# A two-layer decoder trunk on one Trainium2 core: a place of its own for one half's residual, and later transposes, sums and gates in the convolution layer

## The chip, the cores and the metric

The kernel runs on one core of a Trainium2 chip. The metric is the device time of one execution in microseconds (us). A core has five engines that each work through their own list of instructions in order: TensorE (PE; its weight loads are shown as PEld), VectorE (DVE), ScalarE (ACT), GpSimd (POOL) and SyncE (SP), which here issues the DMAs. They meet through semaphores. A measurement of this kernel tells a difference of about 0.2% from none.

## What is computed

The input is 1024 tokens of 1024 channels in float32. Two layers follow each other; each has a token mixer and a feed-forward part with squared ReLU, and each of these four is followed by a residual and a layer norm. The first layer's mixer is a gated recurrence (HGRN2). The change lies in the second layer, whose mixer is a causal convolution module:

```python
u = h @ w_pw1 + b_pw1
a, gate = jnp.split(u, 2, axis=-1)
u = a * jax.nn.sigmoid(gate)
u = lax.conv_general_dilated(u, w_dw[:, None, :], ..., feature_group_count=D_MODEL) + b_dw   # 31 taps per channel
u = jax.nn.silu(layer_norm(u, ln_g, ln_b))
mix = u @ w_pw2 + b_pw2
x = layer_norm(DEEPNORM_ALPHA * x + mix, ln_mix_g[i], ln_mix_b[i])
ff = jnp.square(jax.nn.relu(x @ ffn_w1[i])) @ ffn_w2[i]
x = layer_norm(DEEPNORM_ALPHA * x + ff, ln_ffn_g[i], ln_ffn_b[i])
```

## The kernel before

Float32 products are made of three matmuls: every operand is split into a high part and a remainder (`split`: a cast on ACT, a subtraction on VectorE). A call of `product` (L327) issues one group of them into a PSUM bank, 24 matmuls of 128 x 512 for eight channel blocks or 12 for four. The two feed-forward parts use Strassen-like forms: sums and differences of weight blocks, some of which are formed on POOL by `pool_sums` (L443). That routine loads four weight blocks into four buffers, adds them in four steps and stores each result to DRAM.

The tokens are worked on in two halves of 512. `SEQ` (L38) is an order written by hand in which the stages of the second layer follow each other; a letter names the stage and the digit the half, the channel block or the chunk:

- `P0`, `P1` (`pointwise`, L1140): the gated first product of a channel block of the first and second half. It starts a convolution job: 19 taps on VectorE (`convolve`, L1188) and 12 whose products are scaled on ACT and added on POOL (`convolve_pool`, L1167); the two sums are added at L1204.
- First half: each convolved block is transposed back on TensorE and copied (`back`, L1219), so that tokens stand in the partitions, into the tile `ct[0]`. `N0` (`normalise`, L1236) applies the mean and deviation. `F0` (`finish`, L1301) transposes block by block again, applies gain, bias and silu and splits the result into `sT[0]` (`one(j)` for the eight blocks j). After the last block the residual `kept[0]`, stored in DRAM earlier, is loaded by four DMAs into `ct[0]` (L1318), one for each block of 128 tokens. `S0` (`second`, L1322) scales it and adds the bias (L1327), multiplies `sT[0]` by `w_pw2`, adds the products (L1349), normalises (`norm`, L721) and transposes the outcome into `x3T[0]` (`back` at L1333).
- Second half: the sums stay with the channels in the partitions, in `ct[1]` (`by_channel`, L1185). For their statistics TensorE transposes pairs of blocks into PSUM, where VectorE reads them (`measured`, L1207). `F1` (`second_half`, L1264) queues `stats` (the averages of L1255, with a power on POOL at L1260), `spread` (two groups of matmuls that spread the mean and the scale over the partitions, then eight multiplications on VectorE and eight additions on POOL, L1284, and at the end one `pool_sums` for a chunk of `w2`, L1286) and the silu of block pairs. `S1` is the second product of that half; it reads its residual from `ct[1]` again (L1296).
- `UA` and `UB`: up-projection of the second feed-forward part for the two halves, `V`, `W`, `X`, `Z` parts of its last two chunks in Strassen form. Before `UB0` the sums of `w1b` for these chunks are formed with `pool_sums` (L1524), whose copies read a column of `x3T[1]`.

`ct[0]` lies at 32 KB and `ct[1]` at 48 KB of each partition (L1136). The working order between engines is set by three things. A planner in the kernel (`Background`, L204) keeps estimated clocks of TensorE, VectorE and POOL. After each `product` it runs one entry of a list of chores (`bg.chore`), then steps of the convolution jobs as far as the clocks allow (`bg.pump`). A list `late` holds transposes to be issued inside a later convolution job, at its 6th (first half) or 10th tap (second half). Beyond that, the framework places every instruction in its engine's fixed list by its own schedule, where a later instruction that is expected to be ready may pass an earlier one. To hold a DMA back, the kernel writes one column of its target by a small POOL copy that reads the thing to wait for; `pool_sums` does so with its argument `after` (L449).

Of the kernel before, what the change touches and what calls it, by code (L numbers as in the profile page):

```python
# [8 lines left out]
F32 = mybir.dt.float32  # L9
# [6 lines left out]
P = 128  # L16
D = 1024
S = 1024
KB = D // P
H = 8  # L20
HT = 512
NTB = HT // P
# [238 lines left out]
def body(ctx, tc, d, out):  # L261
    nc = tc.nc
# [29 lines left out]
    def raws(kbs, name="raw"):  # L292
        return ring(kbs, (1024,), name)
# [21 lines left out]
    bg = Background()  # L315
    vector = Clocked(nc.vector, bg.dve, vector_cost)
    tensor = Clocked(nc.tensor, bg.pe, tensor_cost)
# [46 lines left out]
    ident = cst.tile([P, P], F32, name="ident")  # L364
# [325 lines left out]
    def half_stats(bs, yt, j):  # L690
        vector.bn_stats(bs[:, j], yt[:, j * HT : (j + 1) * HT])
# [79 lines left out]
    for half in range(2):  # L771
        for t in range(NTB):
            gates(1, half, t, ws)
        for h in range(H):
            pt = aux()
# [357 lines left out]
    big = Room(((144, 176), (216, 220)), {"u": ((PAD + HT,), 6), "r": (wide_t, 2), "cb": (wide_t, 4), "prod": (wide_t, 3), "z": (wide_t, 2), "halo": ((KB, PAD), 1)})  # L1133
    cvs = bank((3, 7))
    halo = big("halo")
    ct = [view(32 + 16 * h, (NTB, D), F32, "y") for h in range(2)]  # L1136
    cs, conv, pooled, late = [None, None], [], [], []
    taken, turned, gate, normed = [0], [0], [None, []], [0]

# [43 lines left out]
                yield  # L1183

    def by_channel(j):  # L1185
        return ct[1][:, j // 2, j % 2 * HT : (j % 2 + 1) * HT]

    def convolve(half, j, u, sums, other):  # L1188

        while half > normed[0]:  # L1190
            yield WAIT
        ca = cvs()
        if gate[1]:
            nc.vector.tensor_copy(out=ca[:, :1], in_=gate[1].pop())
        nc.scalar.activation(ca, u[:, :HT], AF.Identity, bias=par[:, BDW + j : BDW + j + 1], scale=tap(j, 0))  # L1195
        for i in range(1, TAPS - NPOOL):
            if i == (10 if half else 6):
                while late:
                    late.pop(0)()
            vector.scalar_tensor_tensor(out=ca, in0=u[:, i : i + HT], scalar=tap(j, i), in1=ca, op0=ALU.mult, op1=ALU.add)  # L1200
            yield
        bg.flush(other)
        cb = sums["cb"]
        vector.tensor_tensor(out=by_channel(j) if half else cb, in0=ca, in1=cb, op=ALU.add)  # L1204
        yield

        def measured():  # L1207

            if j == 1:
                cs[1] = stat.tile([P, NTB, 4, 6], F32, tag="cs", name="cs", bufs=1)  # L1210
            for t in range(0, NTB, 2):
                pt = rings["aux"]().rearrange("p (a b) -> p a b", a=2)
                for a in range(2):
                    for b in range(2):
                        tensor.transpose(pt[:, a, b * P : (b + 1) * P], by_channel(j - 1 + b)[:, (t + a) * P : (t + a + 1) * P], ident)
                for a in range(2):
                    vector.bn_stats(cs[1][:, t + a, j // 2], pt[:, a])

        def back():  # L1219
            pt = aux()  # L1220
            for t in range(NTB):
                tensor.transpose(pt[:, t, :], cb[:, t * P : (t + 1) * P], ident)
            nc.scalar.copy(out=ct[half][:, :, j * P : (j + 1) * P], in_=pt)
            turned[0] += 1
            if j % 4 == 3:
                if j == 3:
                    cs[half] = stat.tile([P, NTB, 4, 6], F32, tag="cs", name="cs", bufs=1)[:, :, :2]
                for t in range(NTB):
                    half_stats(cs[half][:, t], ct[half][:, t, :], j // 4)

        if half:
            turned[0] += 1
        if half == 0 or j % 2:
            late.append(measured if half else back)

    def normalise(half):  # L1236

        for job in conv[KB * half : KB * half + KB]:
            bg.flush(job)
        if half == 1:  # L1240
            return
        while late:
            late.pop(0)()
        mv = averages(half)
        normed[0] = 1
        gate[1] = [mv[:, 0, 4:5]] * 2
        for n in range(2):
            for t in range(NTB):
                cv = ct[half][:, t, n * HT : (n + 1) * HT]
                if n == 0 and t % 2:  # L1250
                    vector.tensor_scalar(out=cv, in0=cv, scalar1=mv[:, t, 3:4], scalar2=mv[:, t, 4:5], op0=ALU.mult, op1=ALU.add)
                else:
                    nc.scalar.activation(cv, cv, AF.Identity, bias=mv[:, t, 4:5], scale=mv[:, t, 3:4])
# [10 lines left out]
    def second_half():  # L1264

        at = {}

        def stats():
            while late:
                late.pop(0)()  # L1270
            at["mv"] = averages(1)

        def spread():

            for i, name in ((3, "scale"), (4, "mean")):
                at[name] = pt = banks[:, (3, 7)[i - 3]]
                for t in range(NTB):
                    tensor.matmul(pt[:, t * P : (t + 1) * P], at["mv"][:, t, i : i + 1].to_broadcast([P, P]), ident, start=True, stop=True)
            m = big("z")
            nc.scalar.copy(out=m, in_=at["mean"])  # L1280
            for j in range(KB):
                c = by_channel(j)
                vector.tensor_tensor(out=c, in0=c, in1=at["scale"], op=ALU.mult)
                nc.gpsimd.tensor_tensor(out=c, in0=c, in1=m, op=ALU.add)  # L1284

            pool_sums(*to_sum.pop(0), raws((144, 148, 152, 161), "four"))  # L1286

        def one(j):
            c, sg = by_channel(j), big("r")
            gj, bj = par[:, CLG + j : CLG + j + 1], par[:, CLB + j : CLB + j + 1]  # L1290
            nc.scalar.activation(sg, c, AF.Sigmoid, bias=bj, scale=gj)
            nc.scalar.activation(c, c, AF.Identity, bias=bj, scale=gj)
            vector.tensor_tensor(out=c, in0=c, in1=sg, op=ALU.mult)
            split(sT[1][:, 0, j, :], sT[1][:, 1, j, :], c)
            if j % 2:
                nc.sync.dma_start(out=ct[1][:, j // 2, :], in_=kept[1][j // 2])  # L1296

        nothing = lambda: None
        bg.chores += [stats, spread, nothing, *(lambda j=j: (one(j), one(j + 1)) for j in range(0, KB, 2))]

    def finish(half):  # L1301

        st = sT[half]

        def one(j):
            pt = rings["aux"]()
            for t in range(NTB):
                tensor.transpose(pt[:, t * P : (t + 1) * P], ct[half][:, t, j * P : (j + 1) * P], ident)
            z = big("z")
            sg = big("r")  # L1310
            gj, bj = par[:, CLG + j : CLG + j + 1], par[:, CLB + j : CLB + j + 1]
            nc.scalar.activation(sg, pt, AF.Sigmoid, bias=bj, scale=gj)
            nc.scalar.activation(z, pt, AF.Identity, bias=bj, scale=gj)
            vector.tensor_tensor(out=z, in0=z, in1=sg, op=ALU.mult)
            split(st[:, 0, j, :], st[:, 1, j, :], z)
            if j == KB - 1:
                for t in range(NTB):
                    nc.sync.dma_start(out=ct[half][:, t, :], in_=kept[half][t])  # L1318

        bg.chores += [lambda j=j: (one(j), one(j + 1)) for j in range(0, KB, 2)]  # L1320

# [168 lines left out]
    for op, i in steps:  # L1490
# [9 lines left out]
        if op in ("P0", "P1"):  # L1500
            pointwise(int(op[1]), i)
        elif op == "N":
            normalise(i)
        elif op == "F":
            if i == 1:

                rings["aux"] = bank((0, 4, 3, 7))
            second_half() if i else finish(i)
        elif op == "S":
            second(i)  # L1510
        elif op == "UA":
            up_half(1, i, 0, wa, stA, x3T[0])
        elif op in AHEAD:
            late_ahead(i, AHEAD[op])
        elif op == "Z":
            late_rest()
        else:
            if i == 0:
                wa.raws = raws((184, 188))
                drop(wa_last[1])  # L1520

                four = raws((132, 136, 140, 216), "four")
                for c in range(LATE):
                    pool_sums("w1b", 0, c, four, x3T[1][:, 1, KB - 1, 3 * P - 1 : 3 * P].bitcast(F32))  # L1524
                wa.plan([form("w1b", 0, c, j) for j in LATE_ORDER for c in range(LATE)])
                stB = {"hr": ring(run(0, 2, 16), (8, 2, 256), "hb"), "r": ring(run(128, 2, 2), wide_t, "r"), "t": ring(run(112, 4, 4), (2, 2, 256), "ht")}
            if i == 2:
                x4 += ring((132, 136, 140, 216), (2, HT), "x4", F32R).views
                tmp = ring(run(176, 4, 2), wide_t, "xt")
                for k in range(4):  # L1530
                    bg.chores += x3_differences(k, tmp)
            up_half(1, i, 1, wa, stB, x3T[1])


    y = ct
# [95 lines left out]
```

## Time and profile before

| | us |
|---|---|
| three runs, median | 2132.28 |
| lowest and highest of them | 2131.18, 2132.79 |
| the profiled execution | 2131.32 |
| its span, first to last instruction | 2129.5 |
| TensorE busy in it | 2108.3 |
| VectorE, ACT, POOL busy | 1534.3, 971.4, 451.5 |

A line of the timeline gives the start in us from the beginning of the span, the time until the last of its instructions has ended, the engine, the line of the kernel (L196 and L77 are helpers through which many operations go), the operation, what it writes and reads by tile names, their shapes, and how many instructions were merged (x). Brackets at the end hold the idle time of the engine just before and what ended it. Tiles have names of their own in it: `xa` and `xb` are the split inputs (`x2T`, `sT`) of the two halves, `xc` is `x3T[1]`, `y` stands for `ct`, `four` for the buffers of `pool_sums`, `cb` for POOL's convolution sum. SPq and POOLq rows are DMA issues.

### The profile page before, as it was taken

Reading aid. Unit: us, or ns where it says so; the run is one execution under the profiler, and the core shown is the slowest. Engines: PE = TensorE matmul, PEld = TensorE weight load, DVE = VectorE, ACT = ScalarE, POOL = GpSimd, SP = SyncE. Lnnn points to the kernel's source line nnn. Section 1 sums busy time; section 2 is a strip of 40 time slices with the busy share of each in tenths; the row PEclk is TensorE's granted clock in tenths of the full one; section 3 lists DMA queues with packets and bytes.
Section 4 is the critical chain, followed back from the end, with each engine's and each line's share of the span. In section 5 each row is a group of like instructions: output and inputs, shape, how many; then the busy total and the mean of one; then the engine's idle time right before and its main releaser. Section 6 shows DMA issues by size and latency. Waiting matters only on the chain. (4 is left out here: it accounts for less than half of the span.)

```text
span 2129.5 us, 27331 instructions
## 1 busy us (share of the span) xinstructions
PE 2108.3 (99%) x10136; PEld 1753.2 (82%) x10136; DVE 1534.3 (72%) x2208; ACT 971.4 (46%) x1370; POOL 451.5 (21%) x405
## 2 busy tenths in 40 slices
PE   8999999999999999999999999999999999999998
PEld 7888888888888888888888888888788888888887
DVE  7568898877777666656666798799957946765456
ACT  4222332232266555544444676557444445534333
POOL 0001121123100000000001599189513200040002
PEclk9999999999999999999999999999999999999999
DMA  5567867854248767899998755564585997996642
GB/s 185 144 159 175 229 178 180 232 157 176 92 144 295 268 229 258 310 372 325 339 337 308 292 193 183 208 247 168 194 299 196 335 349 263 370 341 219 192 163 99
DMA packets 166118, 500.76 MB, mean 235 GB/s; under 512 B 15840, under 2 KB 45792, under 8 KB 164704
## 3 DMA queue, kind: packets, MB, share of 16 engines
q1 hardware_dynamic: 159264, 473.85, 63.1%
q0 software_dynamic: 6720, 25.17, 6.7%
q8 instruction: 79, 1.29, 0.2%
q14 instruction: 55, 0.45, 0.1%
HBM read 364.73 MB, written 184.55 MB: 258 GB/s over the span
## 5 line engine op out<-in xcount | busy, mean ns | idle before, releaser
L196 PE MATMUL ps<-dw,dh 128*128 128x512 f32 x2688 | 611.0, 389 | 0.0
L196 PEld LDWEIGHTS ps<-dw,dh 128*128 128x128 f32 x2688 | 504.1, 188 | 104.5
L196 PE MATMUL ps<-x1f,fw 128*128 128x512 f32 x1344 | 305.3, 389 | 0.0
L196 PEld LDWEIGHTS ps<-x1f,fw 128*128 128x128 f32 x1344 | 252.1, 188 | 52.3
L196 PE MATMUL ps<-xa,wa 128*128 128x512 f32 x1152 | 267.5, 391 | 0.0
L196 PEld LDWEIGHTS ps<-xa,wa 128*128 128x128 f32 x1152 | 214.5, 188 | 44.4 <-ACT r L932 0.3
L196 POOL TENSOR_TENSOR cb<-cb,prod 128x512 f32<-128x512 f32 x176 | 234.2, 1340 | 17.8 <-ACT prod L1180 7.1
L196 DVE TENSOR_TENSOR dw<-dr,dw 128x1024 fp32r<-128x1024 f32 x112 | 141.4, 1264 | 97.2 <-ACT dw L77 94.2
L196 DVE TENSOR_TENSOR dh<-dh 128x1024 fp32r<-128x1024 f32 x112 | 140.4, 1256 | 93.7 <-ACT dh L77 93.5
L196 DVE SCALAR_TENSOR_TENSOR ps<-u,par,ps 128x512 f32<-128x512 f32 x288 | 199.6, 752 | 10.9 <-ACT ps L1195 9.4
L196 PE MATMUL ps<-x0T,wa 128*128 128x512 f32 x768 | 189.5, 399 | 6.2 <-ACT x0T L375 6.2
L77 ACT CAST dw<-dr 128x1024 fp32r<-128x1024 f32 x112 | 117.5, 1053 | 156.8 <-PE ps L196 133.8
L77 ACT CAST dh<-dh 128x1024 fp32r<-128x1024 f32 x112 | 117.1, 1050 | 124.9 <-DMA dh<-hf 124.3
L196 PEld LDWEIGHTS ps<-x0T,wa 128*128 128x128 f32 x768 | 142.9, 190 | 35.2 <-ACT x0T L375 6.2
L77 ACT CAST wa<-raw 128x1024 fp32r<-128x1024 f32 (+1 forms) x75 | 76.8, 1026 | 174.4 <-PE ps L196 118.2
L196 PE MATMUL ps<-xc,wa 128*128 128x512 f32 x672 | 153.3, 389 | 0.5 <-DVE wa L196 0.5
L1180 ACT ACTIVATE prod<-u,par 128x512 f32<-128x512 f32 x176 | 125.5, 722 | 56.3 <-POOL cb L196 55.6
L196 PEld LDWEIGHTS ps<-xc,wa 128*128 128x128 f32 x672 | 126.0, 188 | 27.5 <-DVE wa L196 1.3
L196 PE MATMUL ps<-wv,x0T 128*128 128x512 f32 x576 | 140.5, 395 | 0.0
L196 DVE TENSOR_TENSOR wa<-raw,wa 128x1024 fp32r<-128x1024 f32 (+1 forms) x75 | 96.9, 1293 | 58.4 <-ACT wa L77 54.6
L411 POOL TENSOR_TENSOR mv<-mv,nhalf 128x1 f32<-128x1 f32 x32 | 45.6, 1425 | 405.2 <-DVE mv L196 405.2
L196 PEld LDWEIGHTS ps<-wv,x0T 128*128 128x128 f32 x576 | 106.2, 188 | 21.4
(223 smaller groups left out, 2775.7 us busy)
## 6 DMA issues: line engine op xcount, KB each, us to landing
wa<-ready SPq DMA_DIRECT2D x122, 512.0 KB, 4.8
dh<-hf SPq DMA_DIRECT2D x112, 512.0 KB, 5.1
ready<-spare SPq DMA_DIRECT2D x74, 512.0 KB, 4.8
dr<-sum_w SPq DMA_DIRECT2D x64, 512.0 KB, 7.1
sum_w<-in_w_dram SPq DMA_DIRECT2D x24, 1024.0 KB, 8.9
dr<-in_w_dram SPq DMA_DIRECT2D x48, 512.0 KB, 7.6
hf<-ht SPq DMA_DIRECT2D x80, 256.0 KB, 4.1
raw<-in_w1q_dram SPq DMA_DIRECT2D x36, 512.0 KB, 4.0
```

Source lines behind the costliest of these rows:

```text
L77: self.nc.scalar.copy(out=slot[:, 0, c], in_=raw[:, c])
L196: return op(*args, **kw)
L411: nc.gpsimd.tensor_tensor(out=dst, in0=src, in1=nhalf[:, :n], op=ALU.pow)
L1180: nc.scalar.activation(tp, u[:, k : k + HT], AF.Copy, scale=tap(j, k))
```

## The change

Both halves' convolution results now share the place at 32 KB, called `done`; the tile at 48 KB, now `ct[0]`, holds the first half's residual alone, and `ct[1]` is `done`. The residual is loaded after block 3 of `finish` instead of block 7, each of the four loads behind a POOL copy that reads the split of block 3. In the second half, what is in `late` at the 10th tap is appended to the chores instead of being issued there. The `pool_sums` of `w2` gets an `after`: the result of the power in the second half's statistics. The `pool_sums` of `w1b` wait for the transposed second token block of `x3T[1]` instead of the third.

```diff
-    ct = [view(32 + 16 * h, (NTB, D), F32, "y") for h in range(2)]
+
+    done = view(32, (NTB, D), F32, "y")
+    ct = [view(48, (NTB, D), F32, "y"), done]
...
     def by_channel(j):
-        return ct[1][:, j // 2, j % 2 * HT : (j % 2 + 1) * HT]
+        return done[:, j // 2, j % 2 * HT : (j % 2 + 1) * HT]
...
             if i == (10 if half else 6):
+                if half:
+
+                    bg.chores += late
+                    late.clear()
                 while late:
                     late.pop(0)()
...
-            nc.scalar.copy(out=ct[half][:, :, j * P : (j + 1) * P], in_=pt)
+            nc.scalar.copy(out=done[:, :, j * P : (j + 1) * P], in_=pt)
...
-                    half_stats(cs[half][:, t], ct[half][:, t, :], j // 4)
+                    half_stats(cs[half][:, t], done[:, t, :], j // 4)
...
-                cv = ct[half][:, t, n * HT : (n + 1) * HT]
+                cv = done[:, t, n * HT : (n + 1) * HT]
...
-            pool_sums(*to_sum.pop(0), raws((144, 148, 152, 161), "four"))
+            pool_sums(*to_sum.pop(0), raws((144, 148, 152, 161), "four"), at["mv"][:, 0, 3:4])
...
-                tensor.transpose(pt[:, t * P : (t + 1) * P], ct[half][:, t, j * P : (j + 1) * P], ident)
+                tensor.transpose(pt[:, t * P : (t + 1) * P], done[:, t, j * P : (j + 1) * P], ident)
...
-            if j == KB - 1:
+            if j == KB // 2 - 1:
                 for t in range(NTB):
-                    nc.sync.dma_start(out=ct[half][:, t, :], in_=kept[half][t])
+                    nc.gpsimd.tensor_copy(out=ct[0][:, t, :1], in_=st[:, 1, j, :1].bitcast(F32))
+                    nc.sync.dma_start(out=ct[0][:, t, :], in_=kept[0][t])
...
-                    pool_sums("w1b", 0, c, four, x3T[1][:, 1, KB - 1, 3 * P - 1 : 3 * P].bitcast(F32))
+                    pool_sums("w1b", 0, c, four, x3T[1][:, 1, KB - 1, 2 * P - 1 : 2 * P].bitcast(F32))
```

## The prediction

> **What bounds the kernel now.** I read the engine totals first, then the busy time in the stretch that the diff touches, then the timelines around each wait in it.
>
> ```profile
> span 2129.5 us, 27331 instructions
> ## 1 busy us (share of the span) xinstructions
> PE 2108.3 (99%) x10136; PEld 1753.2 (82%) x10136; DVE 1534.3 (72%) x2208; ACT 971.4 (46%) x1370; POOL 451.5 (21%) x405
> ```
>
> ```profile
> 1280.00:1640.00 360.00, 355.32 (x1643) 293.95 (x1642) 290.89 (x406) 199.49 (x308) 207.59 (x153) 1.00 0.59 211
> ```
>
> In the last fence a row is a stretch, its length, the busy time of PE, PEld, DVE, ACT and POOL (instructions in brackets), PE's granted clock, the DMA share and GB/s. TensorE is the bound: it idles 2129.5 - 2108.3 = 21.2 us of the span. The change touches the convolution layer's stretch from 1280 to 1640 us, at full granted clock. There TensorE idles 360.00 - 355.32 = 4.68 us. The diff adds and removes no matmul, so this is nearly all that it can gain, while it can lose more. Four rows of TensorE's timeline, those with an idle time in brackets, hold all of it:
>
> ```profile
> 1373.97 18.00 PE L196 MATMUL ps<-wa,xa 128*128 128x512 f32 x78 [1.10 <-DVE y L196]
> ...
> 1474.53 0.27 PE L196 MATMUL ps<-ident,y 128*128 128x128 f32 x1
> ...
> 1504.64 0.88 PE L196 MATMUL ps<-ident,y 128*128 128x128 f32 x6 [1.95 <-DVE y L196]
> ...
> 1535.96 1.16 PE L196 MATMUL ps<-ident,mv 128*128 128x128 f32 x8 [0.46 <-POOL mv L1260]
> 1538.29 1.16 PE L196 MATMUL ps<-ident,mv 128*128 128x128 f32 x8 [1.17 <-DVE mv L196]
> ```
>
> **The change part by part.** Part 1, the residual. The first half's four loads (L1318) go today into the tile whose last transposes they must wait for. Afterwards they have a place of their own, and each waits for a one-column POOL copy that reads the fourth of the eight silu splits (j = 3).
>
> ```profile
> 1354.93 0.69 DVE L196 TENSOR_TENSOR xa<-z,xa 128x512 fp32r<-128x512 f32 x1
> ...
> 1366.82 1.23 DVE L196 SCALAR_TENSOR_TENSOR y<-y,b_pw 128x1024 f32<-128x1024 f32 x1 [2.08 <-DMA y<-kept]
> 1367.96 0.75 DVE L196 SCALAR_TENSOR_TENSOR ps<-u,par,ps 128x512 f32<-128x512 f32 x1
> 1368.62 0.69 DVE L196 TENSOR_TENSOR xa<-z,xa 128x512 fp32r<-128x512 f32 x1
> 1369.22 1.22 DVE L196 SCALAR_TENSOR_TENSOR y<-y,b_pw 128x1024 f32<-128x1024 f32 x1
> 1370.36 0.69 DVE L196 TENSOR_TENSOR y<-ps,cb 128x512 f32<-128x512 f32 x1
> 1370.96 2.35 DVE L196 SCALAR_TENSOR_TENSOR y<-y,b_pw 128x1024 f32<-128x1024 f32 x2
> 1373.23 2.48 DVE L196 TENSOR_TENSOR y<-y,ps 128x512 f32<-128x512 f32 x4
> ```
>
> ```profile
> 1358.81 0.80 SPq L86 DMA_DIRECT2D wa<-ready  x2
> 1360.98 1.77 SPq L1318 DMA_DIRECT2D y<-kept  x4
> ```
>
> ```profile
> 1384.41 1.52 POOL L411 TENSOR_TENSOR mv<-mv,nhalf 128x1 f32<-128x1 f32 x1 [45.87 <-DVE mv L196]
> ```
>
> The loads issue at 1360.98 and VectorE first gets one at 1366.82, 5.8 us later, having stood idle 2.08. Four scalings (2 x 1.23 + 2.35 = 4.8 us) follow, and only then, at 1373.23, the addition that frees a PSUM bank; TensorE has waited 1.10 for it. Afterwards the j = 3 split ends at 1355.6, the copies add under 1 us (four take 0.54 in a row of part 4) and the loads issue by about 1356.5, so the first lands near 1362.3, 4.5 us sooner. The VectorE idle of 2.08 alone exceeds TensorE's 1.10, so my term is **-1.10**. POOL has been idle for 45.87 us when it comes to 1384.41, so nothing is queued behind these copies; on SP the pair of weight loads at 1358.81 comes behind the residual. Bounds: -1.10, and +1.0 if VectorE, in its fixed order, now stands 2.08 for the landing ahead of the last splits (that of j = 7 is at 1368.62), which the same matmuls need. I take the full gain because those 2.08 us are then no longer spent later.
>
> Sharing one place, the second half's first sum must follow the first half's last transposes. Those end before 1361.0 (the load behind them goes out then) and that sum runs at 1370.36: cost 0, with 9 us of cover.
>
> Part 2, the transposes for the second half's statistics become chores, so they are written one product later (24 matmuls; 18.00 us for 78 in the first row of TensorE's timeline makes that 5.5 us). The stall of 1.95 belongs to six of them.
>
> ```profile
> 1501.90 2.09 DVE L196 TENSOR_TENSOR wa<-raw,wa 128x1024 fp32r<-128x1024 f32 x1 [0.30 <-ACT wa L77]
> 1503.91 0.68 DVE L196 TENSOR_TENSOR y<-ps,cb 128x512 f32<-128x512 f32 x1
> ...
> 1526.77 2.35 DVE L196 TENSOR_TENSOR wa<-raw,wa 128x1024 fp32r<-128x1024 f32 x2
> ```
>
> They start at 1504.64, as the sum at 1503.91 ends. One of the same group ran at 1474.53, 30 us sooner, so the six hang on that sum and not on where they are written; writing them later moves neither the sum nor their place. My term is **0**, between -1.95 (they fall a product later after all) and +1.10 (TensorE arrives sooner by part 1 and the sum does not). The second end I hold for unlikely: the tap chain that leads to the sum starts behind the normalised row of the first half, which TensorE's own products release. What makes the sum late is seen in the first row: a split takes 2.09 us while POOL adds, and 2.35 / 2 = 1.18 when POOL rests. The Trainium skill, "SBUF — State Buffer", section "Who interferes with whom", says that a VectorE instruction with two SBUF inputs and a GpSimd instruction that reads SBUF lock each other out for a whole instruction. The trace agrees (2.09 against 1.18), and by that rule too the stall stays, as the change leaves POOL's convolution adds where they are.
>
> Part 3, the w2 sums (L1286): four POOL copies now wait for the statistics' power (L1260) before the loads may start.
>
> ```profile
> 1530.05 4.87 POOL L453 TENSOR_TENSOR four<-four 128x1024 f32<-128x1024 f32 x2 [20.81 <-DVE cs L196]
> 1534.88 1.03 POOL L1260 TENSOR_TENSOR mv<-mv,nhalf 128x4 f32<-128x4 f32 x1
> 1535.87 5.77 POOL L453 TENSOR_TENSOR four<-four 128x1024 f32<-128x1024 f32 x2
> 1541.60 12.33 POOL L1284 TENSOR_TENSOR y<-y,z 128x512 f32<-128x512 f32 x8
> ```
>
> ```profile
> 1531.02 1.46 DVE L196 TENSOR_SCALAR mv<-mv 128x4 f32<-128x4 f32 x1
> 1535.94 2.29 DVE L196 SCALAR_TENSOR_TENSOR mv<-mv 128x4 f32<-128x4 f32 x1 [3.46 <-POOL mv L1260]
> ```
>
> Today two sums stand ahead of the power: its input is there at 1532.48, it starts at 1534.88, 2.40 late, and everything after it is late by that. The two matmul groups of eight wait 0.46 and 1.17 for it. With the sums behind, the power can end at 1533.5, before 1535.5 where TensorE begins to wait, and the VectorE row that follows (2.29, today beside a sum) ends by 1535.8 at the latest, ahead of the second group's 1537.1. The term is **-1.63**; bounds -1.63 and 0, if TensorE's fixed order asks for the groups as much sooner as they become ready. What is queued behind the copies: on POOL the eight additions (L1284), which need the two matmul groups anyway. The first add can follow the copies by 7.3 us (part 4), near 1541. At worst all four (4.87 + 5.77 = 10.6) stand ahead of the eight, which then start at 1551.5 instead of 1541.6. The last piece made from them is done today 12 us after they end (1553.9):
>
> ```profile
> 1564.64 1.30 DVE L196 TENSOR_TENSOR xb<-y,xb 128x512 fp32r<-128x512 f32 x2
> ```
>
> So of 10 us a few come through at most: cost 0, up to +2. On SP the w2 loads now go out near 1534 behind the copies and later loads queue behind them; TensorE shows no wait for a weight in the stretch, so I count 0.
>
> Part 4, the w1b sums' copies read a column of the second token block instead of the third.
>
> ```profile
> 1624.53 1.03 PE L196 MATMUL ps<-ident,y 128*128 128x128 f32 x8
> ```
>
> ```profile
> 1611.83 1.28 DVE L196 TENSOR_TENSOR xc<-ps,xc 128x512 fp32r<-128x512 f32 x2
> ...
> 1619.85 1.28 DVE L196 SCALAR_TENSOR_TENSOR y<-y,mv,ln_mix_b 128x1024 f32<-128x1024 f32 x1 [0.44 <-POOL mv L411]
> ```
>
> ```profile
> 1618.29 1.52 POOL L411 TENSOR_TENSOR mv<-mv,nhalf 128x1 f32<-128x1 f32 x1 [5.97 <-DVE mv L196]
> 1622.40 0.54 POOL L449 COPY four<-xc 128x1 f32<-128x1 f32 x4 [2.58 <-DVE xc L196]
> 1629.73 11.04 POOL L453 TENSOR_TENSOR four<-four 128x1024 f32<-128x1024 f32 x4 [6.80 <-DMA four<-in_w1b_dram]
> ```
>
> The copies can go at 1613.1 (the split at 1611.83 ends) instead of 1622.4. TensorE does not wait for these sums today, so nothing is gained. But the power of the last row's norm, at 1618.29, now comes after the copies on POOL's one queue. The first add follows the copies by 7.3 us (1622.40 to 1629.73), so near 1620.4, after the power. If the order is power first: **0**. If adds are put ahead of it, it waits for them (first rival). The row ends today at 1621.13 and TensorE asks at 1624.53: 3.4 us of cover, which one add (11.04 / 4 = 2.76) behind a late landing about uses up. Bounds 0 and +9.9 (all four ahead); I take 0.
>
> Sum: -1.10 + 0 - 1.63 + 0 = **-2.73 us**. The profiled execution took 2131.32 (span 2129.5 and 1.8 around it); that gives 2128.6. The median shown, 2132.28, lies 0.96 above that execution, so I predict 2129.6.
>
> **The rivals.**
>
> *POOL's queue at the end of the second product (slower).* Adds of w1b are ordered ahead of the last norm's power, planned with a shorter landing than the chip gives; the 2.08 that VectorE stood for the residual shows such planning. With two ahead the power starts at 1620.4 + 5.5 = 1625.9, the row is ready 1.52 + 1.3 later at 1628.8 and the eight transposes wait 4.3 us beyond 1624.53: 2129.6 + 4.3 = 2133.9, slower. With three, 7.0: 2136.6. It decides from the second add on. Against it: in the profile no add stands ahead of any of the four powers. For it: part 3 shows exactly this on the same engine. Chance 0.28.
>
> *The transposes do get out of the way.* All four waits go: 2132.28 - 4.68 = 2127.6. Chance 0.08; for it only that they are written later.
>
> *The edits do not do what they say.* The residual is late behind something else, or TensorE asks for the statistics as much earlier: one of the two terms is lost, 2130.7 to 2131.2, or both, 2132.3. For it: the order on every engine is fixed ahead, and both gains are waits of 0.5 to 1.2 us. Chance 0.17.
>
> **How the numbers follow.** Forecast 0.45, rivals 0.28, 0.08 and 0.17; 0.02 for worse. A measurement of this kernel tells about 0.2%, 4.3 us, from no change: faster means below 2128.0, slower above 2136.5. The forecast, the third rival and most of the first lie within: same 0.81. Faster needs nearly all 4.68: 0.06. Slower needs three adds or more ahead, or two together with a lost term: 0.13. The range goes from 2127.4 (all waits gone, a fifth of a microsecond for the spread) to 2136.0, the first rival up to nearly three adds; about 0.1 is left above and less below. The likeliest case by itself is 2128.5 to 2131.
>
> **What would show it.** Right: no TensorE wait behind the scalings in the first half's second product; the residual's loads at about 1356.5; the power directly behind its VectorE row and the sums after it; the wait of about 2 us before six transposes still there; the last norm's power still ahead of the w1b adds. Wrong: a TensorE wait on ident,y near 1625 with POOL adds just before it; a wait on xa or wa near 1370; a time below 2128, which would mean that the transposes' wait went too.

## The result and the profile after

| us | before | changed |
|---|---|---|
| median, with lowest and highest (8 runs each) | 2132.28 (2129.56 to 2133.49) | 2137.5 (2135.38 to 2145.36) |
| ratio, 95% interval | | 1.0028 (1.0018 to 1.0039) |
| measured once more (12 and 8 runs) | 2133.7 (2129.88 to 2136.35) | 2138.61 (2136.28 to 2141.8), 1.0026 (1.0016 to 1.0037) |
| profiled execution, its span | 2131.32, 2129.5 | 2139.37, 2137.6 |
| TensorE busy in it | 2108.3 | 2109.6 |

The change makes the kernel slower by 5 to 6 us, where -2.7 was forecast. The time lies above the upper end of the range (2136.0).

TensorE's timeline of the changed kernel, in the stretch that the change touches, answers to the four rows with brackets shown of before (start, time, line, operation, count, and in brackets the idle time before and what ended it):

```profile
1281.10 12.18 PE L196 MATMUL ps<-xb,wa 128*128 128x512 f32 x53
...
1504.52 0.87 PE L196 MATMUL ps<-ident,y 128*128 128x128 f32 x6 [1.85 <-DVE y L196]
...
1534.98 1.95 PE L196 MATMUL ps<-ident,mv 128*128 128x128 f32 x16
1536.68 17.51 PE L196 MATMUL ps<-xa,wa 128*128 128x512 f32 x76
1555.93 5.74 PE L196 MATMUL ps<-xa,wa 128*128 128x512 f32 x24 [1.74 <-ACT r L932]
1565.42 7.11 PE L196 MATMUL ps<-xa,wa 128*128 128x512 f32 x24 [3.75 <-ACT r L932]
1572.37 39.84 PE L196 MATMUL ps<-wa,xb 128*128 128x512 f32 x175
...
1631.70 1.09 PE L196 MATMUL ps<-ident,y 128*128 128x128 f32 x8 [2.09 <-DVE y L196]
```

Of the four waits of before three are gone: the one behind the scalings (1373.97) and the two ahead of the statistics' matmuls, which now run as one row of 16. The one before six transposes stays (1.85, before 1.95). Three new ones stand there: 1.74 and 3.75 in the silu of the second half, 2.09 before the last row's transposes.

Three more rows of before, and one of the changed kernel, complete the marks at which both can be cut:

```profile
1280.11 12.18 PE L196 MATMUL ps<-xb,wa 128*128 128x512 f32 x53
...
1567.44 39.84 PE L196 MATMUL ps<-wa,xb 128*128 128x512 f32 x175
...
1630.86 55.02 PE L196 MATMUL ps<-xc,wa 128*128 128x512 f32 x242
```

```profile
1638.11 2.20 PE L196 MATMUL ps<-xc,wa 128*128 128x512 f32 x9
```

Piece A goes from the x53 row to the first matmul on `mv` (before: 1535.96), B from there to the first on `wa,xb` (the silu of the second half lies in it), C from there to the first on `xc` (the second product of that half and its norm). "Rest" is what follows up to the end of the span.

| us, one profile each | A | B | C | A+B+C | rest |
|---|---|---|---|---|---|
| before | 255.85 | 31.48 | 63.42 | 350.75 | 498.64 |
| changed | 253.88 | 37.39 | 65.74 | 357.01 | 499.49 |

So A gains 1.97, B loses 5.91, C loses 2.32: +6.26 in all. (A second profile of the changed kernel, in the last run below, has +5.02 in all and a rest of 498.75, so the 0.85 of the rest is no steady part of the loss.) The rest loses 0.85 and what precedes the stretch, which the change doesn't touch, is 0.99 longer in this profile; together the 8.1 between the spans. What stands before the stretch varies from profile to profile (its end lies between 1279 and 1287 in the profiles of this study), which is why the pieces tell more here than the medians: in kernels with the same instruction lists A, B and C come back to within some hundredths where no wait on a DMA and no change of clock falls into them.

POOL's timeline of the changed kernel shows what stands where:

```profile
1531.15 1.03 POOL L1266 TENSOR_TENSOR mv<-mv,nhalf 128x4 f32<-128x4 f32 x1 [22.04 <-DVE mv L196]
1532.24 1.58 POOL L449 COPY four<-mv 128x1 f32<-128x1 f32 x4
1539.41 2.41 POOL L453 TENSOR_TENSOR four<-four 128x1024 f32<-128x1024 f32 x1 [5.58 <-DMA four<-in_w_dram]
1541.77 2.54 POOL L1290 TENSOR_TENSOR y<-y,z 128x512 f32<-128x512 f32 x2
1544.27 2.40 POOL L453 TENSOR_TENSOR four<-four 128x1024 f32<-128x1024 f32 x1
1546.61 10.24 POOL L1290 TENSOR_TENSOR y<-y,z 128x512 f32<-128x512 f32 x6
1556.81 5.64 POOL L453 TENSOR_TENSOR four<-four 128x1024 f32<-128x1024 f32 x2
...
1618.18 2.59 POOL L449 COPY four<-xc 128x1 f32<-128x1 f32 x4 [0.93 <-DVE xc L196]
1625.32 2.40 POOL L453 TENSOR_TENSOR four<-four 128x1024 f32<-128x1024 f32 x1 [4.55 <-DMA four<-in_w1b_dram]
1627.67 0.56 POOL L411 TENSOR_TENSOR mv<-mv,nhalf 128x1 f32<-128x1 f32 x1
1628.18 9.06 POOL L453 TENSOR_TENSOR four<-four 128x1024 f32<-128x1024 f32 x3
```

The power (1531.15) now follows its input at once. But one w2 add stands ahead of the eight additions (L1290), one between them, two behind; and one w1b add stands ahead of the last norm's power (1627.67). POOL works without a break from 1539.41 to 1562.45, where before it rested from 1553.93. VectorE in the same time, and at the last scaling:

```profile
1532.21 0.17 DVE L196 SCALAR_TENSOR_TENSOR mv<-mv 128x4 f32<-128x4 f32 x1 [1.15 <-POOL mv L1266]
...
1555.63 4.58 DVE L196 TENSOR_TENSOR xb<-y,xb 128x512 fp32r<-128x512 f32 x2
1560.13 3.46 DVE L196 TENSOR_TENSOR y<-y,r 128x512 f32<-128x512 f32 x2
...
1566.81 0.69 DVE L196 TENSOR_TENSOR y<-y,r 128x512 f32<-128x512 f32 x1 [0.87 <-ACT y L1298]
...
1628.26 3.39 DVE L196 SCALAR_TENSOR_TENSOR y<-y,mv,ln_mix_b 128x1024 f32<-128x1024 f32 x1 [2.51 <-POOL mv L411]
1631.57 0.68 DVE L196 TENSOR_TENSOR xc<-ps,xc 128x512 fp32r<-128x512 f32 x1
1632.17 2.81 DVE L196 TENSOR_TENSOR wa<-raw,wa 128x1024 fp32r<-128x1024 f32 x1
```

The two x2 rows merge unlike pieces: the first is 1.77 and 2.89, the second 2.86 and 0.68. A narrower window shows the two long ones alone:

```profile
1557.32 2.89 DVE L196 TENSOR_TENSOR xb<-y,xb 128x512 fp32r<-128x512 f32 x1
1560.13 2.86 DVE L196 TENSOR_TENSOR y<-y,r 128x512 f32<-128x512 f32 x1
```

So a piece of 128 x 512 with both inputs in SBUF (the core's memory, in which the tiles lie) takes 1.8 us beside one of the eight additions, 2.9 beside an add of w2 and 0.68 when POOL rests. The last scaling takes 3.39 (before 1.28) and the weight split behind it 2.81 beside the adds of w1b (1632.17), but `xc<-ps,xc`, which takes one input from PSUM, keeps its 0.68 beside the same adds (1631.57). ACT's timeline shows how TensorE comes into it:

```profile
1563.03 0.62 ACT L675 CAST xb<-y 128x512 fp32r<-128x512 f32 x1 [4.00 <-DVE y L196]
...
1564.78 0.59 ACT L932 ACTIVATE r<-ps 128x512 f32<-128x512 f32 x1
```

ACT waits 4.00 us for VectorE's product of the silu (the one of 2.86 at 1560.13); behind that cast in its list stands the relu of the up-projection (L932) that empties the PSUM bank which TensorE needs next. TensorE goes on at 1565.42.

### The profile page after: what moved, and what is told of

Same layout as the page of the kernel before. It is cut to its first block, busy times and chain, and to the rows that moved or that the text cites. A ratio compares the mean times of both kernels' runs of the same rounds, so it can differ in the third digit from the quotient of the medians.

```text
span 2137.6 us, 27346 instructions
## 1 busy us (share of the span) xinstructions
PE 2109.6 (99%) x10136; PEld 1754.7 (82%) x10136; DVE 1539.2 (72%) x2208; ACT 971.5 (45%) x1370; POOL 454.7 (21%) x413
## 4 chain that ended last, share of the span: by engine, by line
PE 89%; POOL 3%; DVE 3%; DMA 2%; issue 1%; ACT 1%; SPq 0%; DVEq 0%; POOLq 0%
PE ps L196 89%; POOL cb L196 3%; DVE y L196 1%; DVE ps L196 1%; DMA raw<-in_wg_dram 1%; DVE xb L196 0%; DVE wa L196 0%; DMA raw<-in_wv_dram 0%; DMA four<-in_w_dram 0%; DMA dr<-in_w_dram 0%; DMA dh<-hf 0%; DMA raw<-in_xT_dram 0%; DMA four<-in_w1b_dram 0%; POOL four L449 0%; ACT wv L77 0%
## 5 line engine op out<-in xcount | busy, mean ns | idle before, releaser
L196 DVE TENSOR_TENSOR dh<-dh 128x1024 fp32r<-128x1024 f32 x112 | 144.8, 1296 | 92.4 <-ACT dh L77 87.2
```

The costliest lines, as they stand in the source:

```text
L196: return op(*args, **kw)
```

## The experiments

Theory A: POOL's adds in new places cost the time, those of w2 by about 5 net and those of w1b by about 2; the residual and the chores cost nothing, and the parts add up. Rival B: the w1b gate alone carries the loss, as in the prediction's first rival. Later came rival C, that the loads and stores at new times cost it and not the adds. A1 and A2 are two forms of A: the place in POOL's queue, or VectorE slowed beside POOL. The first four runs, of five rounds each, share one median of before, 2132.93 (33 runs).

**One part alone: the residual.** Of the diff only the tiles and the loads of `finish`.

> Only the residual's new place and its earlier load. Theory A (the loss comes from the gate of the w2 sums) and theory B (it comes from the gate of the w1b sums) both expect the wait of 1.10 us behind the four scalings to be gone and nothing new: 1 us faster than before, 2131.2 beside 2132.3. If the earlier landing had pushed the last splits, a wait of up to 1 us on xa near 1370 would stand in its place and the time would be that of before.

Measured 2132.74, ratio 1.000 (0.999 to 1.001); A 254.52, B 31.48, C 63.42. The wait of 1.10 is gone, nothing is late in its place, yet the time doesn't show the 1 us that was expected. The profiles of the next three runs, which still load the residual the old way, show that this wait was not always there: 0.33 in the first of them (1372.18) and none in the other two, where the first scaling came 4.6 us after the issue instead of 5.84.

**One part alone: the gate of w2.**

```diff
-            pool_sums(*to_sum.pop(0), raws((144, 148, 152, 161), "four"))
+            pool_sums(*to_sum.pop(0), raws((144, 148, 152, 161), "four"), at["mv"][:, 0, 3:4])
```

> Only the w2 sums behind the power. Theory A: the two waits of 0.46 and 1.17 us on mv go, and TensorE waits for ACT's L932 near 1555 and 1562 for 5 us or more, because POOL's four adds now run among the silu's multiplications; 4 to 6 us slower than before, 2137. Theory B: the two waits go and no new one comes: 1.6 us faster, 2130.7.

Measured 2137.68, ratio 1.0014 (1.0004 to 1.0023); A 254.16, B 38.84, C 63.42, +5.67 in the stretch. TensorE's timeline has the two waits again:

```profile
1554.50 5.74 PE L196 MATMUL ps<-xa,wa 128*128 128x512 f32 x24 [1.72 <-ACT r L932]
1563.98 8.27 PE L196 MATMUL ps<-xa,wa 128*128 128x512 f32 x24 [3.75 <-ACT r L932]
```

**One part alone: the gate of w1b** (`3 * P - 1 : 3 * P` becomes `2 * P - 1 : 2 * P`).

> Only the earlier column for the w1b sums. Theory A: one add stands ahead of the last norm's power, six or eight transposes wait about 2 us near 1626, and nothing else changes: 2 us slower than before, 2134.3. Theory B: 5 us slower or more, 2137.5.

Measured 2134.99, ratio 1.0009 (1.0000 to 1.0018); C 66.06, +2.64, with one wait of 2.41 in TensorE's timeline:

```profile
1630.26 1.09 PE L196 MATMUL ps<-ident,y 128*128 128x128 f32 x8 [2.41 <-DVE y L196]
```

**One part alone: the chores** (the four lines in `convolve`).

> Only the transposes as chores. Both theories: the wait of 1.95 us before six transposes stays between 1.8 and 2.0, the time is that of before within 0.5 us, 2132.3. If the chores carried part of the loss, the time would be over 2133.5.

Measured 2131.54, ratio 0.9998 (0.9989 to 1.0007). The wait before the six transposes stays (1.88 at 1504.60). B is falsely short here, 30.55: a slow clock (below) held TensorE back after that wait, so that it came later to the statistics. Rival B falls: w2's gate costs more than w1b's. The four medians lie -0.2, +4.8, +2.1 and -1.4 from that of before, 5.2 together, so the parts add up as far as intervals of some 2 us to either side can tell.

**No sums.** The changed kernel without the adds of these chunks; loads, copies and stores stay.

```diff
-            nc.gpsimd.tensor_tensor(out=a[y], in0=a[x], in1=a[y], op=ALU.add)
+            if adds:
+                nc.gpsimd.tensor_tensor(out=a[y], in0=a[x], in1=a[y], op=ALU.add)
```

> The changed kernel, but the four POOL adds of this chunk of w2 and the adds of the two w1b chunks are left out (the loads, the waiting copies and the stores stay; those sums are then wrong, as this part of the computation is missing). Theory A (the adds on POOL cost the time, by their place ahead of the additions and by what they do to VectorE beside them): the two TensorE waits of about 1.7 and 3.7 us near 1555 and 1565 behind ACT's evacuation (L932) and the 2.1 us before the last row's eight transposes near 1631 are all gone, VectorE's products, remainders and the last scaling take 0.7 and 1.3 us sooner, and the time is about 2130 or a little below. Rival C (the loads and stores that now go out near 1532 and 1618 cost it, by SP's queue or by DMA traffic): the waits stay, and the time is about 2137.

A 253.93, B 29.92, C 63.42: 347.27, 3.48 less than before and 9.74 less than the changed kernel; no new wait is left. The one time, 2133.57, says nothing against it, as its stretch began 6.8 us later than in before (1286.93). Rival C falls. This is also the bottom to measure by: without hindrance B is 29.9 and C 63.4.

**Memsets in place of the adds.** Two memsets of the target for each add; they write SBUF and read nothing of it.

```diff
+            else:
+                for _ in range(2):
+                    nc.gpsimd.memset(a[y], 0.0)
```

> The changed kernel, but each of those twelve POOL adds is replaced by two POOL memsets of the same buffer, which write SBUF and read nothing (the sums are left out, so this part of the computation is missing). Theory A1 (the place in POOL's queue alone costs it): POOL's additions and the last power still stand behind the memsets, so TensorE waits about as much as the memsets last. Theory A2 (mostly VectorE that is slowed while POOL reads SBUF): beside the memsets VectorE's instructions keep 0.7 us (remainders) and 1.3 us (last scaling), and what waits remain are only as long as a power or an addition was late; the last scaling at 1.28 instead of 3.39 alone would take 2.1 us off, so no wait near 1631.

A 255.49, B 29.93, C 63.42; time 2129.86. No new wait is left. POOL and VectorE at the last norm:

```profile
1618.74 2.86 POOL L457 MEMSET four<- 128x1024 f32 x3 [3.26 <-DMA four<-in_w1b_dram]
1621.57 0.55 POOL L411 TENSOR_TENSOR mv<-mv,nhalf 128x1 f32<-128x1 f32 x1
1622.06 4.53 POOL L457 MEMSET four<- 128x1024 f32 x5
```

```profile
1622.15 1.28 DVE L196 SCALAR_TENSOR_TENSOR y<-y,mv,ln_mix_b 128x1024 f32<-128x1024 f32 x1 [3.10 <-POOL mv L411]
```

The power ends 55.0 us after the start of C (1567.09), in the run without sums at 52.4, in the changed kernel at 55.9. So a power late by 2.7 costs nothing, as the cover of 3.4 in the prediction said; it is the scaling of 1.28 that became 3.39 beside adds which turns a used-up cover into a wait of 2.09. Beside memsets it stays 1.28. In the silu the memsets, shorter than the adds, test the place only in part: the eight additions end 18.2 us after the start of B (1537.16 to 1555.34), in the run without sums 15.0, in the changed kernel 21.9. So 3.2 us of delay cost nothing there; the run with the first two adds, below, tests the rest. The Trainium skill, "SBUF — State Buffer", section "Who interferes with whom", says that a VectorE instruction with two SBUF inputs contends with a GpSimd instruction that reads SBUF, not with one that only writes it; the two rows agree (3.39 and 1.28).

**The w2 sums behind the eight additions** (they wait for `by_channel(KB - 1)`; w1b as before the change).

> The changed kernel with the w1b copies back on the third token block, and with the w2 copies waiting for the last of the eight POOL additions (L1290) instead of the power. The power and the additions then go first, and the four w2 adds come about 7 us after the additions' end near 1550, at about 1557 to 1567. Theory A1 (place in the queue): the gain of the power stays, the silu stretch is as in the kernel before, 2129.5 to 2130.5. Theory A2 (VectorE slowed beside any POOL add): the last two block pairs of the silu are still slowed by about 1.4 us an instruction, and one TensorE wait behind L932 of up to 4 us stays: 2131 to 2133.

Measured 2135.94 against 2133.44 (23 runs), ratio 1.0005 (0.9995 to 1.0016); A 255.54, B 29.93, C 63.42. The stretch is free; the rest takes 502.21, with four waits for weights of 0.35 to 1.21 between 1668 and 1705 (next run). VectorE's row for the last pair:

```profile
1558.86 5.44 DVE L196 TENSOR_TENSOR y<-y,r 128x512 f32<-128x512 f32 x2 [0.73 <-ACT y L1298]
```

2.7 us each instead of 0.69, and TensorE doesn't wait in the stretch: the splits of this pair end at 1569.92, after the next stage has begun (1566.27), and are still in time. A2 as I had put it (slowed in any place) is too strong; what counts is whether TensorE soon needs the slowed piece, or an eviction that stands behind it in ACT's list. The waits in the rest had been expected under neither form, and the time is above what both expected.

**The w2 sums behind the silu.**

```diff
-            pool_sums(*to_sum.pop(0), raws((144, 148, 152, 161), "four"), at["mv"][:, 0, 3:4])
+        def sums_of_w2():
+            pool_sums(*to_sum.pop(0), raws((144, 148, 152, 161), "four"), sT[1][:, 1, KB - 1, :1].bitcast(F32))
...
+        bg.chores += [stats, spread, nothing, *(lambda j=j: (one(j), one(j + 1)) for j in range(0, KB, 2)), sums_of_w2]
```

> The changed kernel with the w1b copies back on the third token block, and with the w2 sums issued behind the silu, their copies waiting for the last split of it (near 1565). The adds then run at about 1573 to 1585, where neither TensorE nor the silu needs POOL or VectorE at once. Theory A under either form: the residual's 1.1 us and the 1.6 to 2.3 us of the statistics' matmuls are gained and nothing is given back, so 2129.0 to 2130.0, faster than the kernel before by 0.1 to 0.2 per cent. Rival C (the loads' traffic or SP's queue): a wait of TensorE for a weight or an evacuation after 1565, and about 2132 or more.

The stretch is as expected, 347.24, the time is not: 2134.83 against 2133.44, ratio 1.0005 (0.9994 to 1.0017). The rest takes 503.74, 5.1 more than before. In TensorE's timeline new waits for weights stand there (1.82 at 1669.97, then 1.15 and 0.73 by 1699.66, and a slow clock behind these, at 0.56 and 0.59 from 1700 to 1704):

```profile
1669.97 27.08 PE L196 MATMUL ps<-xc,wa 128*128 128x512 f32 x118 [1.82 <-DVE wa L196]
```

VectorE and POOL before it:

```profile
1662.02 3.43 DVE L196 SCALAR_TENSOR_TENSOR ht<-ht,hb 128x1024 f32<-128x1024 f32 x1
1665.37 3.41 DVE L196 TENSOR_TENSOR ht<-hb 128x1024 f32<-128x1024 f32 x1
1668.71 1.21 DVE L196 TENSOR_TENSOR wa<-raw,wa 128x1024 fp32r<-128x1024 f32 x1
```

```profile
1634.30 10.81 POOL L453 TENSOR_TENSOR four<-four 128x1024 f32<-128x1024 f32 x4 [7.77 <-DMA four<-in_w1b_dram]
...
1658.98 8.72 POOL L453 TENSOR_TENSOR four<-four 128x1024 f32<-128x1024 f32 x3 [1.98 <-DMA four<-in_w1b_dram]
```

The w1b adds begin 4.8 us behind the up-projection's first matmul (1629.46); before they began 1.1 ahead of theirs. They lie beside VectorE's work for the up-projection: two rows take 3.4 instead of 1.2, and the weight split that TensorE waits for stands right behind them. Before has two such rows too (3.42 at 1652.14 and at 1661.11), but 21 and 30 us behind the first matmul, not 33 and 36. The two rows lose 4.4 us, more than the wait of 1.82. So by the rows the gain of the stretch is lost to the same mechanism in the next one; no run leaves out these adds alone.

**The same with the early gate of w1b.** All of the change, but the w2 sums behind the silu.

> The changed kernel with all its parts, the w1b copies on the second token block as the change has them, but with the w2 sums issued behind the silu, as in the run before. The instruction lists put the last norm's power ahead of the first w1b add here, where the changed kernel had one add ahead. Theory A (adds only hurt where they stand ahead of, or beside, a piece that TensorE asks for next): no wait of TensorE in the silu stretch and none near 1625, the stretch from the first product of the fourth block to the up-projection's first matmul takes about 347.3 us (350.75 before, 357.01 in the changed kernel), and with the w1b sums stored earlier the waits for weights between 1669 and 1705, which cost the run before some 5 us, go too: about 2128. Rival D (those later waits come from another order of the DMA queue, whatever the sums do): they stay, and the time is 2132 to 2134.

Measured **2129.62** against 2132.93 (21 runs), ratio **0.9987 (0.9978 to 0.9996)**: below both kernels, though the interval only just excludes no difference; about 2128 had been expected. A 255.51, B 29.93, C 63.42, rest 497.65; the only wait from the x53 row to the end is the old one before the six transposes. POOL's list shows why the early gate does no harm here:

```profile
1618.70 1.52 POOL L411 TENSOR_TENSOR mv<-mv,nhalf 128x1 f32<-128x1 f32 x1 [3.39 <-DVE mv L196]
1620.51 11.57 POOL L453 TENSOR_TENSOR four<-four 128x1024 f32<-128x1024 f32 x4 [0.29 <-DMA four<-in_w1b_dram]
```

The power comes first, and the adds begin 9.5 us ahead of the up-projection's first matmul (1630.05), in the run before 4.8 behind it, so that less of them lies beside the up-projection.

**w1b behind the last power itself.** As the run behind the silu, with the result of that power as `after`.

> As the run with the sums behind the silu, but the w1b copies wait for the result of the last norm's power itself, so that no add of theirs can stand ahead of it. Theory A: the first w1b add comes near 1625, about 9 us sooner than with the third token block (1634.3), TensorE keeps 347.3 us for the stretch, and the waits for weights after 1669 shrink from 3.7 us to under 1: 2128 to 2129.5. Rival D (order of the DMA queue): they stay, 2132 to 2134. Against theory A too: a TensorE wait near 1625 behind VectorE's last scaling, which then runs beside the first add (2 us more), would show that the place of an add beside VectorE costs by itself.

Rival D is that the waits for weights come from another order of the DMA queue. Measured 2133.97, ratio 1.0003 (0.9994 to 1.0012): the time that was expected under rival D, not under theory A. The stretch is 347.25, but one wait of 2.49 for a weight stands at 1679.88, a slow clock follows it, and the rest is 501.98. The adds begin 3.6 us ahead of the up-projection's first matmul (1624.22 against 1627.82), in the run before 9.5. That alone doesn't explain the wait, as in the kernel before the change they begin 1.1 ahead and its waits there are 0.32 and 0.18. Against rival D stands that VectorE is busy for 24.68 of the 25 us from 1655 to 1680 and that no row of VectorE or ACT in that time waits for a DMA. Whether another order of VectorE's rows brings the wait was not tried; its cause stays open.

**The first two adds only.** The changed kernel, w1b as before the change, without the two w2 adds that follow the eighth addition.

> The changed kernel with the w1b copies back on the third token block, and of the four w2 adds only the first two, which stand among the additions in POOL's list as in the changed kernel; the last two, which there follow the eighth addition, are left out (so two of these sums are missing). Theory A1 (it is the place of the first two, ahead of and between the additions): both waits behind L932 stay, or one wait of about the same sum, since the additions start as late as in the changed kernel. Theory A2 (it is VectorE, slowed by the two adds that follow, beside the third block pair's products and remainders): the wait of 3.75 near 1565 is gone, with the slow clock behind it, and at most the one of 1.74 near 1556 stays, so the silu stretch costs 30 to 32 us instead of 37.4.

B 31.28: one wait of 1.06 is left, the one of 3.75 is gone, with the slow clock behind it. The additions end 21.2 us after the start of B, nearly as late as in the changed kernel, so their place (A1) explains this 1.06 at most. Of the 7.46 by which B lies above 29.93 in the changed kernel, 1.35 comes from the two adds ahead of and among the additions, and 6.1 (1.4 of it slow clock) from the two that follow them. It is not the place of these two: POOL has nothing behind them until 1604.64 in the changed kernel. The pieces that take 2.89 and 2.86 there, the last remainder of the second pair of blocks and the first product of the third, take 0.68 each here.

**The changed kernel again.**

> The changed kernel once more, on the chip of this comparison. By the theory its three waits (about 1.7, 3.7 and 2.1 us) are set by its instruction lists and come again in every profile, while the slow clock after a wait need not: 2136 to 2139, 1.002 to 1.004 of the kernel before.

Measured as in the first table. A 253.92, B 36.10, C 65.75: the waits come again as 1.77, 2.09 and 2.10. The second, expected at about 3.7 again, was 3.75 in the first profile; here the slow clock came after the first wait and had TensorE arrive later, so it waited less. It goes on 30.6 us after the start of B here and 30.4 there: VectorE sets that.

## Why the prediction was wrong

- **Part 1** (-1.10): the mechanism was right, the loads went out at 1357.28 and no wait came in its place. The size was that of one profile. Three others of the old way show 0.33, 0 and 0, since the landing varies; 1.10 was the largest of four, and "I take the full gain" was too much. Sharing one place cost nothing, as said.
- **Part 2** (0): right. The six transposes hang on the sum ahead of them, 1.85 to 1.95 in all 14 profiles.
- **Part 3, the gain** (-1.63): right: the row of VectorE after the power took 0.17 instead of 2.29 (1532.21) and both groups run without a wait.
- **Part 3, the cost**: this is the step that failed: "So of 10 us a few come through at most: cost 0, up to +2." It took the 12 us between the additions' end and the last piece for the slack of all pieces. The third pair of blocks has little: ACT's list holds the up-projection's eviction behind it, and VectorE, slowed from 0.68 to 2.9 beside the adds of w2, makes ACT late. POOL is busy until 27.5 us after the start of B instead of 18.0, so more of VectorE's rows are slowed. B lost 7.46 against its bottom: 1.74 and 3.75 of waits, 1.4 of slow clock (7.11 against 5.74 for 24 matmuls), and about 0.3 more at each of the two waits, as in the run with the first two adds (1.06 of wait, 1.35 of loss). The slowing was in the prediction's own rows (2.09 and 1.18 in part 2) and was not applied to the silu.
- **Part 4 and the first rival**: the rival's mechanism came about (a wait on `ident,y` with POOL adds before it, at 1631.70), though the forecast held it for 0.28 likely. But "It decides from the second add on" was wrong: one add was ahead, its 3.5 us used up the cover, and the scaling's extra 2.11 beside the next adds made the wait of 2.09.

By the pieces: -1.97 + 5.91 + 2.32 = +6.26 in the first profile and +5.02 in the second, instead of -2.73. Of "what would show it", the wait near 1625 was named; the waits behind L932 were not.

## What to carry to other kernels

When work on POOL is moved, list every VectorE instruction with two SBUF inputs that will lie beside it, price each at the slowed duration, and follow each into the list of the engine that waits for it: what stands behind that wait may be the eviction of another stage. Slack is to be read for each piece, not for the last one. And a wait that ends with a DMA's landing is worth what several profiles show, not one.

## What the runs showed of the hardware

A wait of TensorE can cost more than itself. TensorE's granted clock (third number from the end) behind the wait of 3.75 in the changed kernel, and behind the wait of 1.90 in the run with the sums behind the additions:

```profile
1564.00:1566.00 2.00, 0.58 (x1) 0.50 (x2) 1.94 (x3) 2.00 (x5) 0.00 (x0) 0.74 0.98 369
1566.00:1568.00 2.00, 2.00 (x6) 1.60 (x5) 1.19 (x2) 2.00 (x5) 0.00 (x0) 0.50 0.93 328
1568.00:1570.00 2.00, 2.00 (x9) 1.61 (x9) 1.92 (x4) 1.73 (x4) 0.00 (x0) 0.90 1.03 424
```

```profile
1504.27:1506.27 2.00, 2.00 (x10) 1.77 (x11) 1.43 (x3) 1.50 (x3) 1.84 (x3) 0.75 0.72 213
1506.27:1508.27 2.00, 2.00 (x6) 1.52 (x6) 2.00 (x4) 1.97 (x3) 1.92 (x2) 0.50 0.12 49
1508.27:1510.27 2.00, 2.00 (x10) 1.61 (x9) 2.00 (x2) 1.23 (x3) 0.56 (x1) 0.90 0.00 0
```

If the clock is either full or half, 0.74, 0.50 and 0.90 over 2 us each make 1.04 + 2.0 + 0.4 = 3.4 us at half, and so does the second fence. Behind the wait of 3.75 in the run with w2's gate alone it lasted twice that, 6.8 us (0.65, 0.50, 0.50 and 0.65 from 1562 to 1570). It costs about half of that: the second run's A is 1.65 longer than that of the run behind the silu (253.89). After the same wait of 1.85 to 1.95 the slow clock came in 4 of 14 profiles. The best kernel's profile is one of these four (A 255.51), so its 2127.7 of span holds 1.6 that another execution need not pay. The Trainium skill, "TensorE: Matmul & The Clock Gate", section "What's actually happening", gives a free-running window of 3413 ns; the 3.4 us and the chance nature agree. The same page of the Trainium skill, section "Why this matters for your kernels", warns of idle gaps over about 3 us; here 1.9 were enough in some profiles, as were 1.77 in the second profile of the changed kernel, and the measurement decides.
